# One subtraction and one clamp for eight heads in a Mamba-2 scan, and later stores of the second layer's weight pairs

## The chip, the cores and the metric

The kernel runs on one core of a Trainium2 chip. The metric is the device time of one execution in microseconds. Three runs of the kernel before took 3096.12, 3100.96 and 3102.59 us; the median is 3100.96.

## The reference

The model has two layers over 2048 tokens of width 1024. The first is a Mamba-2 mixer with 32 heads of width 64 in 4 groups and a state of 128; the second is multi-head latent attention with 16 heads, whose keys and values come from a latent of width 256. The part that the change touches in the first layer is the decay inside a chunk of the scan:

```python
cum = jnp.cumsum(dt_c * A_g, axis=1)
seg = cum[:, :, None] - cum[:, None, :]
L = jnp.exp(jnp.where(causal, seg, -jnp.inf))
CB = jnp.einsum('btgn,bsgn->btsg', C_c, B_c)
y_intra = jnp.einsum('btsg,btsgh,bsgh,bsghp->btghp', CB, L, dt_c, x_c)
```

The part that it touches of the second layer are that layer's weights: `w_dkv` (1024 x 288), `w_in` (1024 x 1408, the query latent and the gate), `w_ukv` (256 x 2048) and `w_uq` (384 x 1536). The reference multiplies with them in fp32.

## The kernel before

The kernel goes through the first layer in 16 items: four token blocks of 512 (b), and in each the four groups (g). An item has the projections (`xbc`, `zgate`), the scan (`ssd`) and the output projection (`outp`). The scan of one item is a generator that is advanced between the steps of the other parts, so that TensorE gets products of the projections between those of the scan. Then come the second layer's projections (`mla`), the attention (`attention`), whose TensorE order is written out by hand, and the last projection (`back`). Outside the attention a planner, which counts costs and priorities, sets the order of each engine's instructions when the kernel is built; on the chip each engine, SP's queue among them, keeps its order, and an instruction that waits holds up those behind it.

**The scan's differences (lines 829 to 845).** The scan of an item has four chunks of 128 tokens, 64 chunks in all. For each, SP fetches the rows of the cumulated decay of eight heads, spread over all partitions, into the tile E (tag `big`, two buffers, 128 x 8 x 128; line 831). VectorE subtracts from each head's 128 columns that head's column of `cum`, one value per partition, and clamps at zero from below (line 843, eight instructions). ScalarE takes the exponential (line 844), VectorE multiplies by CB (line 845), and TensorE takes E as weights of 16 products (line 870). Behind them lie y (lines 871 to 878), its square (880), a power of two from the square (883 to 885), the scaling of y (900) and its transpose (812).

**The second layer's weight pairs (lines 424 to 502).** Products with fp16 operands are made of pairs, a high and a low half, and the pairs of the second layer's weights are made in the background of the first layer's last two blocks, in 49 pieces of up to 512 columns. A piece is a raw load on SP (line 437, one piece ahead of its use), the high half on ScalarE and the low half on VectorE (`pair16`, lines 119 and 120), and a store of the pair to DRAM on SP (line 439). Raw weights and pairs share the five buffers of the tag `wraw`. `owed` holds pairs that are made and not yet stored. `make` runs most pieces; `value_weights` makes those of the value part of `kv_w_up`, which also yield a vector of powers of two, stored to `us_d` (line 493). Its pairs are stored at line 502, the first store of each of its two rounds at line 473, and the last store of all at line 461.

On the same SP queue stand the loads of the first layer's pairs (`wi_d`, line 230, and `wo_d`, line 694) and of the decay rows (line 831). ScalarE also empties the banks of `xbc` into `craw` (line 610), which frees the bank for the next products; line 781 is a small Exp for the chunks' end weights.

Of the kernel before, what the change touches and what calls it, by code (L numbers as in the profile page):

```python
# [10 lines left out]
F32 = mybir.dt.float32  # L11
# [5 lines left out]
ALU = mybir.AluOpType  # L17
# [4 lines left out]
P = 128  # L22
# [49 lines left out]
class Net:  # L72
# [352 lines left out]
    def second_weights(self):  # L425

        yield from self.second_powers()
        a = self.a
        owed = []

        def make(todo):
            raws = []
            for m, (src, gain, d) in enumerate(todo):
                while len(raws) < min(m + 2, len(todo)):
                    raws.append(self.t(self.wp, "wraw", [P, TB], bufs=WRAW))
                    ahead = todo[len(raws) - 1][0]
                    self.nc.sync.dma_start(raws[-1][:, :ahead.shape[1]], ahead)
                if owed:
                    self.nc.sync.dma_start(*owed.pop())
                n = src.shape[1]  # L440
                u = self.t(self.wp, "wraw", [P, 2, n], F16, bufs=WRAW)
                self.pair16(u[:, 0], u[:, 1], raws[m][:, :n], gain)
                owed.append((d, u))
                yield

        def rows(w, k, c0, n):
            return w[k * P:(k + 1) * P, c0:c0 + n]

        w_in = a["mla_w_in"]
        todo = [(rows(w_in, k, 384, TB), self.g1u[:, k:k + 1], self.wg_d[0][k]) for k in range(KD)]  # L450
        todo += [(rows(a["kv_w_down"], k, 0, 288), self.gku[:, k:k + 1], self.wd_d[k]) for k in range(KD)]
        todo += [(rows(w_in, k, 0, 384), self.g1u[:, k:k + 1], self.wq_d[k]) for k in range(KD)]
        todo += [(rows(a["kv_w_up"], k, n * TB, TB), self.gklu[:, k:k + 1], self.wu_d[n][k])
                 for n in range(2) for k in range(2)]
        yield from make(todo)
        yield from self.value_weights(owed)
        todo = [(rows(a["mla_w_uq"], k, n * TB, TB), self.gqu[:, k:k + 1], self.wu_d[4 + n][k])
                for n in (2, 0, 1) for k in range(3)]
        todo += [(rows(w_in, k, 384 + TB, TB), self.g1u[:, k:k + 1], self.wg_d[1][k]) for k in range(KD)]
        yield from make(todo)  # L460
        self.nc.sync.dma_start(*owed.pop())
        yield

    def value_weights(self, owed):

        nc, v = self.nc, self.nc.vector
        for n in range(2):
            cs = slice(1024 + n * 512, 1536 + n * 512)
            raw = [self.t(self.wp, "wraw", [P, TB], bufs=WRAW) for _ in range(2)]
            for k in range(2):  # L470
                nc.sync.dma_start(raw[k], self.a["kv_w_up"][k * P:(k + 1) * P, cs])
            if owed:
                nc.sync.dma_start(*owed.pop())
            yield
            u = [self.t(self.wp, "wraw", [P, TB], F32R, bufs=WRAW) for _ in range(2)]
            for k in range(2):
                nc.scalar.activation(u[k], raw[k], AF.Abs, scale=self.gkl[:, k:k + 1])
            yield
            ps = self.t(self.pp, "tr", [P, TB], bufs=4)
            for k in range(2):  # L480
                nc.tensor.matmul(ps, self.ones_r, u[k], start=k == 0, stop=k == 1)
            x = self.t(self.sp, "cacc", [P, TB], bufs=2)
            v.tensor_scalar(x, ps, TINY, None, ALU.max)

            e = self.t(self.sp, "craw", [P, TB], I32, bufs=3)
            v.tensor_scalar(e, x.bitcast(I32), 23, None, ALU.logical_shift_right)
            f = self.t(self.sp, "cacc", [P, TB], I32, bufs=2)
            v.tensor_scalar(f, e, -1, 264, ALU.mult, ALU.add)
            v.tensor_scalar(f, f, 23, None, ALU.logical_shift_left)
            v.tensor_scalar(e[0:1], e[0:1], -25, None, ALU.add)  # L490
            v.tensor_scalar(e[0:1], e[0:1], 23, None, ALU.logical_shift_left)
            v.tensor_scalar(e[0:1].bitcast(F32), e[0:1].bitcast(F32), self.gdown[0:1], None, ALU.mult)
            nc.sync.dma_start(self.us_d[n * 512:(n + 1) * 512], e[0:1, :].bitcast(F32))
            for k in range(2):
                nc.gpsimd.tensor_tensor(raw[k], raw[k], f.bitcast(F32), ALU.mult)
            yield
            for k in range(2):
                w = self.t(self.wp, "wraw", [P, 2, TB], F16, bufs=WRAW)
                self.pair16(w[:, 0], w[:, 1], raw[k], self.gklv[:, k:k + 1])
                owed.append((self.wu_d[2 + n][k], w))  # L500
                yield
                nc.sync.dma_start(*owed.pop())

    def second_powers(self):

# [283 lines left out]
    def ssd(self, b, g):  # L789

        nc, v, act = self.nc, self.nc.vector, self.nc.scalar.activation
        dt, cum, ecum, dec, wend, cumT = self.dtv[b]
# [27 lines left out]
        for c in range(4):  # L820
            s = slice(c * P, (c + 1) * P)
            h0 = c * H + g * 8
# [7 lines left out]
            E = self.t(self.sp, "big", [P, D], bufs=2).rearrange("p (h t) -> p h t", h=8)  # L830
# [8 lines left out]
                Ct = halves(pair("Ct", P, 2), CT[:, s])  # L839
            CB = self.t(self.sp, "CB", [P, P], bufs=2)  # L840
            v.tensor_tensor(CB, pb[:, P:2 * P], self.triu, ALU.mult)
            for h in range(8):
                v.tensor_scalar(E[:, h, :], E[:, h, :], cum[:, h0 + h:h0 + h + 1], 0.0, ALU.subtract, ALU.max)
            act(E, E, AF.Exp, scale=-1.0)
            v.tensor_tensor(E, E, CB.unsqueeze(1).to_broadcast([P, 8, P]), ALU.mult)
            yield
# [34 lines left out]
            if b:  # L881
                e = self.t(self.sm, "pwe", [P, 1], I32)
# [627 lines left out]
```

## Time and profile before

| | |
|---|---|
| median of three runs | 3100.96 us |
| profiled execution | 3099.32 us, its span 3097.2 us |
| mean granted TensorE clock | 0.995 |
| TensorE (matmul) busy | 2994.5 us, 97% |
| VectorE busy | 2330.1 us, 75% |
| ScalarE busy | 1936.4 us, 63% |
| GpSimd busy | 615.3 us, 20% |

Busy time is the union of the instructions' spans on an engine. A mean duration of one instruction also holds its passage through a pipeline, so that a row of instructions back to back takes less than their number times the mean. A wait is put down to the releaser that came last. Waits of SP are those of the queue that issues transfers.

### The profile page before, as it was taken

Reading aid. Unit: us, or ns where it says so; the run is one execution under the profiler, and the core shown is the slowest. Engines: PE = TensorE matmul, PEld = TensorE weight load, DVE = VectorE, ACT = ScalarE, POOL = GpSimd, SP = SyncE. Lnnn points to the kernel's source line nnn. Section 1 sums busy time; section 2 is a strip of 40 time slices with the busy share of each in tenths; the row PEclk is TensorE's granted clock in tenths of the full one; section 3 lists DMA queues with packets and bytes.
Section 4 is the critical chain, followed back from the end, with each engine's and each line's share of the span. In section 5 each row is a group of like instructions: output and inputs, shape, how many; then the busy total and the mean of one; then the engine's idle time right before and its main releaser. Section 6 shows DMA issues by size and latency. Waiting matters only on the chain.

```text
span 3097.2 us, 51355 instructions
## 1 busy us (share of the span) xinstructions
PE 2994.5 (97%) x17758; PEld 1759.2 (57%) x17758; DVE 2330.1 (75%) x5306; ACT 1936.4 (63%) x4920; POOL 615.3 (20%) x842
## 2 busy tenths in 40 slices
PE   7899999999999999999999999999999999999998
PEld 3466655555455554545555555456666666665777
DVE  7789887777777687797755453488888888888576
ACT  8777566665667656565534333388888888888422
POOL 0211122211222112222111212322122222222100
PEclk9999999999999999999999999999999999999999
DMA  8675436445454466364466555622223222232485
GB/s 298 221 235 181 151 106 220 129 158 163 153 191 162 131 207 222 121 199 145 145 214 197 194 173 170 197 49 60 55 56 67 54 58 57 54 88 75 130 261 158
DMA packets 205065, 457.11 MB, mean 148 GB/s; under 512 B 28114, under 2 KB 57554, under 8 KB 203364
## 3 DMA queue, kind: packets, MB, share of 16 engines
q1 hardware_dynamic: 176948, 375.94, 37.9%
q0 software_dynamic: 27856, 77.89, 9.8%
q8 instruction: 140, 2.29, 0.3%
q14 instruction: 121, 0.99, 0.1%
HBM read 340.99 MB, written 112.73 MB: 146 GB/s over the span
## 4 chain that ended last, share of the span: by engine, by line
PE 40%; DVE 5%; ACT 4%; issue 3%; DMA 2%; POOL 0%; SPq 0%; ACTq 0%; POOLq 0%; DVEq 0%
PE mm L88 7%; PE mm L90 6%; PE mm L89 6%; PE tr L1248 6%; PE tr L1259 3%; PE tr L1258 3%; PE tr L88 3%; PE tr L90 3%; PE tr L89 3%; ACT Pr L1233 2%; DVE PTs L120 1%; DMA os<-ri_d 1%; ACT PTs L119 1%; DVE mx L1221 1%; PE mm L1220 0%
## 5 line engine op out<-in xcount | busy, mean ns | idle before, releaser
L120 DVE SCALAR_TENSOR_TENSOR PTs<-tr,PTs 128x512 f16<-128x512 f32 (+3 forms) x640 | 374.2, 606 | 76.8 <-ACT PTs L119 69.7
L1233 ACT ACTIVATE Pr<-mm,nm 128x512 f32<-128x512 f32 (+2 forms) x631 | 394.2, 635 | 49.4 <-DVE nm L1225 44.9
L1221 DVE TENSOR_REDUCE mx<-mm 128x1 f32<-128x512 f32 (+2 forms) x631 | 373.1, 604 | 31.1 <-PE mm L90 28.3
L119 ACT ACTIVATE PTs<-tr 128x512 f16<-128x512 f32 (+3 forms) x640 | 329.4, 544 | 97.9 <-PE tr L1248 95.9
L1248 PE MATMUL tr<-pack,Pr 128*128 128x128 f32 x2176 | 317.5, 273 | 1.8 <-ACT Os L1265 1.4
L88 PE MATMUL mm<-xT,wsp 128*128 128x512 f16 x800 | 305.7, 382 | 7.9 <-ACT wsp L119 4.9
L89 PE MATMUL mm<-xT,wsp 128*128 128x512 f16 x800 | 304.6, 381 | 0.0
L90 PE MATMUL mm<-xT,wsp 128*128 128x512 f16 x800 | 303.6, 380 | 0.0
L1248 PEld LDWEIGHTS tr<-pack,Pr 128*128 128x128 f32 x2176 | 253.2, 141 | 68.9 <-ACT Os L1265 2.2
L88 PE MATMUL mm<-K,xT 96*128 96x512 f16 (+2 forms) x639 | 222.4, 348 | 27.5 <-ACT Pr L1233 24.0
L88 PE MATMUL mm<-wsp,xT 128*128 128x512 f16 (+1 forms) x640 | 232.0, 363 | 4.3 <-ACT craw L610 4.1
L89 PE MATMUL mm<-wsp,xT 128*128 128x512 f16 (+1 forms) x640 | 232.3, 363 | 3.0 <-DVE wsp L120 3.0
L89 PEld LDWEIGHTS <-xT 128*128 128x128 f16 (+1 forms) x1408 | 138.0, 98 | 168.1 <-issue 69.6
L616 DVE SCALAR_TENSOR_TENSOR cacc<-craw,pack,cacc 128x512 f32<-128x512 f32 x288 | 219.3, 790 | 18.0 <-ACT cacc L614 17.2
L90 PE MATMUL mm<-wsp,xT 128*128 128x512 f16 (+1 forms) x640 | 232.5, 364 | 0.0
L90 PE MATMUL mm<-K,xT 96*128 96x512 f16 (+2 forms) x639 | 221.8, 347 | 0.0
L89 PE MATMUL mm<-K,xT 96*128 96x512 f16 (+2 forms) x639 | 221.2, 346 | 0.0
L1258 PE MATMUL tr<-PTs,xT 128*128 128x512 f16 (+3 forms) x640 | 221.0, 347 | 0.1
L1259 PE MATMUL tr<-PTs,xT 128*128 128x512 f16 (+3 forms) x640 | 219.1, 347 | 0.0
L90 PEld LDWEIGHTS <-xT 128*128 128x128 f16 (+1 forms) x1408 | 136.9, 97 | 133.1 <-issue 5.7
L88 PEld LDWEIGHTS <-xT 128*128 128x128 f16 (+1 forms) x1408 | 137.7, 98 | 120.1 <-issue 8.5
L88 PE MATMUL mm<-wsp,yT 128*128 128x512 f16 (+1 forms) x512 | 197.4, 385 | 0.9 <-DVE sz L640 0.5
(456 smaller groups left out, 6795.8 us busy)
## 6 DMA issues: line engine op xcount, KB each, us to landing
wsp<-wi_d SPq DMA_DIRECT2D x96, 512.0 KB, 3.6
big<-cumT SPq DMA_DIRECT2D x64, 512.0 KB, 4.8
wraw<-in_ssm_w_out_dram SPq DMA_DIRECT2D x96, 256.0 KB, 3.6
wi_d<-wsp SPq DMA_DIRECT2D x32, 512.0 KB, 3.8
wsp<-wo_d SPq DMA_DIRECT2D x32, 512.0 KB, 3.5
wsp<-wu_d SPq DMA_DIRECT2D x28, 512.0 KB, 3.8
hx<-in_ssm_w_in_dram SPq DMA_DIRECT2D x48, 256.0 KB, 4.8
wraw<-in_ssm_w_in_dram SPq DMA_DIRECT2D x48, 256.0 KB, 4.4
```

The lines of the kernel that those rows point to most:

```text
L88: mm(out, l_hi, r_hi, start=start, stop=False)
L89: mm(out, l_hi, r_lo, start=False, stop=False)
L90: mm(out, l_lo, r_hi, start=False, stop=stop)
L119: self.nc.scalar.activation(hi, src, AF.Copy, scale=scale)
L120: self.nc.vector.scalar_tensor_tensor(lo, src, scale, hi, ALU.mult, ALU.subtract)
L616: nc.vector.scalar_tensor_tensor(acc, raw[:, k:k + TB], wk[k], acc, ALU.mult, ALU.add)
L1221: v.tensor_reduce(mx[:, n:n + 1], s[:, :w], AX.X, ALU.max)
L1233: nc.scalar.activation(x[:, :w], s[:, :w], AF.Exp, bias=nm, accum_out=sm[:, n:n + 1])
L1248: nc.tensor.transpose(pt[:, j * P:(j + 1) * P], st["P"][j][kb], self.ident)
L1258: nc.tensor.matmul(st["O"][:, c], vals[h][:, kb, :], u[:, 0], start=kb == 0, stop=False)
L1259: nc.tensor.matmul(st["O"][:, c], vals[h][:, kb, :], u[:, 1], start=False, stop=kb == nk - 1)
```

## The change

In the scan the eight instructions of line 843 become two for all eight heads: a subtraction of a tensor from a tensor, in which each head's column of `cum` is repeated over 128 elements, and a clamp at zero in place.

In `make`, a pair is stored only when more than one is owed, and then the oldest; before, the one owed was stored at the next piece. After the last piece all that are owed are stored. In `value_weights`, all owed pairs are stored once the raw loads of a round are issued; its own pairs are no longer stored right after they are made but with the next round or the next pieces; and the store of `us_d` is issued one step later.

```diff
-                if owed:
-                    self.nc.sync.dma_start(*owed.pop())
+                if len(owed) > 1:
+                    self.nc.sync.dma_start(*owed.pop(0))
...
         yield from make(todo)
-        self.nc.sync.dma_start(*owed.pop())
+        while owed:
+            self.nc.sync.dma_start(*owed.pop(0))
         yield
...
-            if owed:
-                nc.sync.dma_start(*owed.pop())
+            while owed:
+                nc.sync.dma_start(*owed.pop(0))
             yield
...
-            nc.sync.dma_start(self.us_d[n * 512:(n + 1) * 512], e[0:1, :].bitcast(F32))
             for k in range(2):
                 nc.gpsimd.tensor_tensor(raw[k], raw[k], f.bitcast(F32), ALU.mult)
             yield
+            nc.sync.dma_start(self.us_d[n * 512:(n + 1) * 512], e[0:1, :].bitcast(F32))
             for k in range(2):
                 w = self.t(self.wp, "wraw", [P, 2, TB], F16, bufs=WRAW)
                 self.pair16(w[:, 0], w[:, 1], raw[k], self.gklv[:, k:k + 1])
                 owed.append((self.wu_d[2 + n][k], w))
                 yield
-                nc.sync.dma_start(*owed.pop())
...
-            for h in range(8):
-                v.tensor_scalar(E[:, h, :], E[:, h, :], cum[:, h0 + h:h0 + h + 1], 0.0, ALU.subtract, ALU.max)
+            v.tensor_tensor(E, E, cum[:, h0:h0 + 8].unsqueeze(2).to_broadcast([P, 8, P]), ALU.subtract)
+            v.tensor_scalar(E, E, 0.0, None, ALU.max)
             act(E, E, AF.Exp, scale=-1.0)
```

## Rows read from the trace of the kernel before

**Rows 1.** Busy time by stretch: the scan layer, the pieces' part, the attention.
```profile
core 0: us, PE busy (x) PEld busy (x) DVE busy (x) ACT busy (x) POOL busy (x), PEclk, DMA share, GB/s
35.00:1560.00 1525.00, 1483.17 (x8902) 805.69 (x8901) 1208.33 (x2717) 972.08 (x2483) 312.05 (x381) 0.99 0.53 174
1090.00:1410.00 320.00, 306.57 (x1816) 157.32 (x1814) 265.17 (x608) 189.56 (x470) 70.67 (x79) 0.99 0.58 191
2010.00:3098.00 1088.00, 1046.07 (x6400) 707.56 (x6397) 879.00 (x2059) 774.65 (x2084) 199.29 (x289) 1.00 0.35 87
```

**Rows 2.** Waits of PE in 35 to 1560: total us, times, longest.
```profile
PE tr L812 <- ACT y L900: 9.1, 7, 2.7
PE mm L88 <- ACT craw L610: 5.8, 4, 3.1
```

**Rows 3.** Instruction groups by shape: busy us, mean ns, idle before.
```profile
L843 DVE TENSOR_SCALAR big<-big,d_cum 128x128 f32<-128x128 f32 x512 | 136.6, 314 | 38.5 <-DMA big<-cumT 38.3
...
L845 DVE TENSOR_TENSOR big<-big,CB 128x1024 f32<-128x1024 f32 x64 | 78.0, 1219 | 0.8
...
L578 DVE TENSOR_SCALAR hx<-hx,rsy 128x1024 f32<-128x1024 f32 x24 | 16.5, 749 | 0.2
...
L981 DVE TENSOR_SCALAR yt<-yt 128x512 f32<-128x512 f32 x4 | 1.7, 426 | 0.1
```

**Rows 4.** Timeline of DVE at 1349: start, us, instruction, idle before.
```profile
1349.22 1.66 DVE L843 TENSOR_SCALAR big<-big,d_cum 128x128 f32<-128x128 f32 x8 [1.83 <-DMA big<-cumT]
```

**Rows 5.** Timeline of DVE at 1190 to 1193.
```profile
1190.24 0.29 DVE L843 TENSOR_SCALAR big<-big,d_cum 128x128 f32<-128x128 f32 x1 [0.94 <-DMA big<-cumT]
...
1191.04 0.15 DVE L883 TENSOR_SCALAR pwe<-ms 128x1 int32<-128x1 int32 x1
...
1193.04 0.28 DVE L843 TENSOR_SCALAR big<-big,d_cum 128x128 f32<-128x128 f32 x1
```

**Rows 6.** Waits of SP's queue in 1048 to 1410.
```profile
SPq L439 <- DVE wraw L120: 37.3, 23, 5.2
SPq L502 <- DVE wraw L120: 7.5, 4, 4.0
SPq L493 <- DVE craw L492: 7.2, 1, 7.2
...
SPq L437 <- DMA wu_d<-wraw: 4.7, 5, 2.3
```

**Rows 7.** Timeline of SP's queue, 1324 to 1356.
```profile
1332.78 0.33 SPq L437 DMA_DIRECT2D wraw<-in_mla_w_uq_dram  x1
...
1342.98 0.45 SPq L831 DMA_DIRECT2D big<-cumT  x1
...
1354.86 0.38 SPq L437 DMA_DIRECT2D wraw<-in_mla_w_uq_dram  x1
```

**Rows 8.** Timeline of ACT, 1349 to 1352.
```profile
1349.95 0.72 ACT L119 ACTIVATE wraw<-wraw,gains 128x512 f16<-128x512 f32 x1 [2.21 <-DMA wraw<-in_mla_w_uq_dram]
1350.92 1.06 ACT L844 ACTIVATE big<-big 128x1024 f32<-128x1024 f32 x1 [0.25 <-DVE big L843]
1351.88 0.67 ACT L610 ACTIVATE craw<-mm,down 128x512 f32<-128x512 f32 x1
```

**Rows 9.** Timeline of PE, 1348 to 1356.
```profile
1352.60 0.38 PE L88 MATMUL mm<-wsp,xT 128*128 128x512 f16 x1 [3.15 <-ACT craw L610]
...
1354.49 0.38 PE L88 MATMUL mm<-wsp,xT 128*128 128x512 f16 x1 [0.44 <-ACT craw L610]
```

**Rows 10.** Timeline of ACT, 1117 to 1124.
```profile
1120.49 0.53 ACT L119 ACTIVATE wraw<-wraw,gains 128x288 f16<-128x288 f32 x1 [2.65 <-DMA wraw<-in_kv_w_down_dram]
```

**Rows 11.** Timeline of PE, 1120 to 1124.
```profile
1123.38 1.04 PE L870 MATMUL tr<-Xd,big 128*64 128x64 f32 x28 [2.44 <-issue]
```

**Rows 12.** The tile wraw in 1090 to 1410: who waited for it, landing times.
```profile
  ACT wraw L119: 33.8, 24
...
DMA to landing us min/median/max: 1.7/3.3/6.5
```

## The prediction

> **What bounds the kernel now.** I read the busy times by stretch first. In the scan layer, 35 to 1560 us, TensorE is busy 1483 of 1525 us at a granted clock of 0.99, VectorE 1208, ScalarE 972; in the attention stretch behind it, which the change doesn't touch, TensorE is busy 1046 of 1088 [rows 1]. So the scan layer is TensorE's: what the change can win in it is at most the 42 us in which TensorE stands idle there, and both edits lie on engines with room (VectorE idles 317 us of the stretch). The waits of TensorE come next: the largest two groups are a transpose that waits for ScalarE's last scaling of y (9.1 us in 7 waits) and a product that waits until ScalarE has emptied a bank into craw (5.8 us in 4) [rows 2]. Neither names the edited lines, so I looked for what stood in front of those ScalarE instructions in their queue. In the stretch in which the second layer's weights are made, 1090 to 1410, TensorE idles 13.4 us [rows 1], and its two longest waits there that lead to the edited work are followed below.
>
> **The scan's decay differences: operations.** The eight subtract-and-clamp instructions of a chunk have a mean duration of 314 ns [rows 3], but that is not what eight of them take: they are pipelined, and where nothing stands between them all eight end 1.66 us after the first has begun [rows 4]. They go, and one 128x1024 subtraction of two tensors comes, with a clamp of 128x1024 behind it that reads what the subtraction writes. The subtraction is in kind, width, type and in having one broadcast operand the multiplication of line 845, 1219 ns. The clamp has two near rows: 426 ns for 128x512 without a per-partition operand, 749 ns for 128x1024 with one [rows 3]. So a chunk costs between 1.22 + 0.43 = 1.65 us and 1.22 + 0.75 = 1.97 us in place of 1.66. I take the upper end, since that row has the width of the clamp: 0.31 us more for a chunk, 64 chunks, 20 us more of VectorE in a stretch where it idles 317.
>
> The Trainium skill ("VectorE: DVE Perf Modes", the section on the TRN2 errata) counts a VectorE instruction between SBUF operands as 58 cycles of 0.96 GHz plus its elements, divided by two where fp32 has one tensor operand. Worked out from that page as an estimate, eight small ones are 1.02 us and the new pair 1.72 us, so its rule speaks against the edit more strongly (0.70 us for a chunk, 45 us over 64), although the same section advises few large instructions over many small ones. The trace doesn't agree with it for the small ones, which take 1.66 us [rows 4]; by the page the scan half below would cost some 5 us in place of 2.
>
> **The scan half on the path.** The chain of a chunk is: cumT's rows land, differences, Exp, multiplication, TensorE's 16 products, y, the square, the power of two, the scaling, the transpose. TensorE waits for its end in 7 of 64 chunks [rows 2]; in the others it has other products, and VectorE's extra time is covered. If all 7 shift by 0.31 us the price is 2.2 us; I take 2. The bounds come from the other form in which the eight occur: the planner puts short instructions between them. From 1190.24 to 1193.32 the eight took 3.08 us, with the power-of-two chain of the chunk before (line 883) between [rows 5]. The new pair would give Exp its input 1.1 us sooner there, and 7 such chunks are worth -8 us. On the other side, line 883 stood behind one piece of 0.29 us; behind a subtraction of 1.22 us it would start 0.93 us later, and 7 times that is +6.5 us. The 38.3 us in which VectorE waits at the differences for cumT's rows [rows 3] stay whichever form waits.
>
> **The stores.** The same 49 stores of pairs and the same bytes are issued on SP; only their place changes. Before, the store of a piece stands right behind the next piece's load, and SP, which works in order, waits there for VectorE's low half: 37.3 us in 23 waits, 7.5 us in 4 at the value weights' own stores, and 7.2 us in one at the store of us_d [rows 6]. With one more piece between, the halves have long been made, so I put nearly all of the 37.3 and 7.5 at nothing, and the store of us_d behind one more piece. SP waits by themselves cost nothing; what stands behind them does: loads of raw weights, loads of cumT's rows and of the first layer's pairs.
>
> Where does that reach TensorE? First at 1352.60: it waited 3.15 us, then 0.44 us, for craw [rows 9]. ScalarE was free to empty the bank only at 1351.88, because it had stood 2.21 us at a raw weight that had not landed, and then did the Exp of a chunk [rows 8]. VectorE in turn had begun that chunk's differences at 1349.22 after 1.83 us of waiting for cumT's rows [rows 4], which SP had issued at 1342.98 [rows 7]. That is the train of loads that started only at 1332.78 [rows 7], when SP had come out of its 7.2 us at us_d [rows 6]. Starting it even 2 to 3 us sooner takes both waits away: -3.6 us. Second at 1123.38: TensorE stood 2.44 us [rows 11] because ScalarE had stood 2.65 us at a raw weight of the pieces, in front of a small Exp that the chunk needed [rows 10]. That load stood behind SP's store waits too: -2.4 us. Behind either the next late thing is the same ScalarE queue, which then has no gap; the other waits of the stretch (13.4 - 3.6 - 2.4 = 7.4 us) I leave. At the end, two stores in place of one are flushed; nothing stands behind them but first-layer loads, and I put that at nothing (0.4 us if SP were late then).
>
> What it costs is space. Five buffers hold raw weights and pairs alike. With one pair more held back, the next raw load finds free only the buffer of the piece just converted or that of a pair whose store was issued one piece before. Where that store hasn't landed, the wait comes back at the load (before, 4.7 us in 5 waits for one of the stored tensors [rows 6]). I take nothing for it in the forecast; its bound is the rival below.
>
> **Sum.** The profiled execution took 3099.3 us (span 3097.2). 3099.3 - 3.6 - 2.4 + 2 = 3095.3, so 3095, against the median of the three runs, 3101, a gain of 0.2%. Its own range, with half or none of the second term and the scan half between -2 and +4, is 3090 to 3101.
>
> **Rivals.**
> (a) *The ring of five becomes the bound: slower.* Place: the raw loads of the pieces. In the densest train nine loads went out between 1332.78 and 1354.86 [rows 7], one every 2.5 us, while a store's landing takes 3.3 us in the median [rows 12]. It decides where pieces follow each other closer than a store lands: then each load waits for the store before it, 0.8 us more, and 45 loads make 36 us. ScalarE stands at raw weights 33.8 us now [rows 12], and of that 5.6 us (3.15 + 2.44) came through to TensorE, one sixth; 36 us more would bring 6, neither gap would go, and with the scan's 2 the time is 3107 to 3108. For it: loads wait for stored tensors even now [rows 6]. Against it: the other free buffer, that of the piece just converted, may be taken, and over the whole stretch 49 pieces are made in 320 us, one in 6.5.
> (b) *The waits only change hands.* SP is free sooner, but the loads behind are held by TensorE's use of the buffers, or ScalarE meets its next late input: both gaps stay, the scan's 2 us are added: 3101. For it: both raw-weight waits shown end with a landing [rows 8, 10], and that the issue was late is my inference. Against it: SP's 7.2 us at us_d lead straight to the gap at 1352.60.
> (c) *The shorter path through the differences pays*: the -8 us above in place of +2: 3085. For it: interleaved runs of the eight as in [rows 5] exist. Against it: VectorE's work grows, and TensorE names none of these lines as its releaser.
>
> **How the numbers follow.** Forecast 0.48, (a) 0.24, (b) 0.16, (c) 0.12. A measurement of this kernel tells 0.2%, 6 us, from no change, so faster is below 3095 and slower above 3107. The forecast lies on that border: I give 0.27 of its 0.48 to faster and 0.21 to the same. With 0.11 of (c), faster is 0.38; with 0.19 of (a) and 0.03 of (b), slower is 0.22; the rest, 0.40, is the same. The range takes in (c) nearly and (a) with some room above: 3084 to 3112.
>
> **What would show it.** Right: the 1.83 us at the differences and the 2.21 us at the raw weight in that train gone, SP's waits at line 439 near nothing, the pair at 1.9 to 2.0 us per chunk, TensorE idle under 8 us between 1090 and 1410. Wrong: SP's waits at line 437 for stored tensors above 30 us and ScalarE's at raw weights above 50 (a); TensorE's idle time in 35 to 910 moved by more than 5 us, which only the scan half can do. If TensorE's idle time moves as much outside the named places as in them, the planner's new order and not these steps made the time, and the working above is wrong even where the time fits.

## The result and the profile after

The changed kernel took 3105.99 us in the median of 22 runs (3099.46 to 3111.57), the kernel before 3100.39 in as many beside it. The ratio is 1.0019, with a 95% interval of 1.0012 to 1.0025: 5.6 us slower, where 3095 and a gain had been forecast. The profiled execution took 3107.3 us (span 3105.5; before 3099.3 and 3097.2).

Busy time by stretch in the kernel after, for [rows 1]:

```profile
35.00:1560.00 1525.00, 1480.34 (x8868) 802.20 (x8867) 1219.18 (x2336) 971.86 (x2483) 323.81 (x381) 0.99 0.53 174
1090.00:1410.00 320.00, 304.84 (x1823) 157.23 (x1818) 264.88 (x518) 189.66 (x471) 71.23 (x80) 0.98 0.58 188
2010.00:3098.00 1088.00, 1054.42 (x6438) 711.95 (x6435) 878.72 (x2050) 775.96 (x2086) 202.22 (x293) 1.00 0.36 88
```

VectorE's busy time in the scan layer rose by 10.9 us (1208.3 to 1219.2), half of the 20 that I had counted. TensorE still idles 44.7 us there (1525 less 1480.3; before 41.8) and 15.2 in the pieces' part (before 13.4; forecast under 8). The third row holds 8 us more TensorE work than before because the layers ahead of it ended later. Idle time is not all of the loss: over the whole execution TensorE's 17758 products were busy 2999.2 us, before 2994.5, so that 4.7 of the 8.3 us by which the span grew are longer products. The mean granted clock of the profiled execution was 0.994, before 0.995.

TensorE's waits in 35 to 1560 after, for [rows 2]:

```profile
PE tr L812 <- ACT y L900: 12.9, 8, 4.5
PE mm L88 <- ACT craw L610: 6.2, 5, 2.9
```

The wait for y's last scaling grew from 9.1 to 12.9 us, and its longest from 2.7 to 4.5.

The differences by shape after, for [rows 3] (subtraction in line 842, clamp in 843):

```profile
L842 DVE TENSOR_TENSOR big<-big,d_cum 128x1024 f32<-128x1024 f32 x64 | 81.7, 1276 | 35.0 <-DMA big<-cumT 34.6
...
L843 DVE TENSOR_SCALAR big<-big 128x1024 f32<-128x1024 f32 x64 | 48.7, 761 | 0.2
```

Undisturbed, the two take 1.22 and 0.69 us (the medians are 1224 and 686 ns), so 1.91 for a chunk, as forecast.

SP's waits in 1048 to 1410 after, for [rows 6] (line 439 is the store of a pair, 437 the load of a raw weight, 497 the store of us_d, 472 the load of a raw value weight):

```profile
SPq L437 <- DVE wraw L120: 33.5, 12, 5.0
SPq L439 <- DVE wraw L120: 11.3, 9, 2.8
SPq L497 <- DVE craw L493: 7.5, 1, 7.5
...
SPq L472 <- DVE wraw L120: 4.9, 2, 3.7
SPq L437 <- DMA wd_d<-wraw: 4.7, 3, 1.7
```

The store's wait of 37.3 us shrank to 11.3, but the load that stands ahead of it took over 33.5 us of the same wait, for VectorE's low half (before, 3.5 us at the load). us_d still holds SP for 7.5 us. SP's waits at line 437 for stored tensors did not grow (15.1 us for all four tensors after, 15.5 before).

The tile wraw in 1090 to 1410 after, for [rows 12]:

```profile
  ACT wraw L119: 39.9, 31
...
DMA to landing us min/median/max: 1.9/3.5/6.5
```

ScalarE waited 39.9 us there, 33.8 before, and these waits are of several kinds. The largest of ScalarE's own list of waits in that stretch, for raw loads and for pairs on their way to DRAM:

```profile
ACT wraw L119 <- DMA wraw<-in_mla_w_in_dram: 10.6, 6, 3.5
ACT wraw L119 <- DMA wg_d<-wraw: 6.8, 5, 2.4
...
ACT wraw L478 <- DMA wu_d<-wraw: 4.0, 2, 2.0
ACT wraw L119 <- DMA wu_d<-wraw: 3.9, 3, 2.5
```

For raw loads line 119 waited 15.6 us, 17.1 before. For a buffer whose stored pair had not landed ScalarE waited 18.4 us (line 478, where the value weights are made, with it), 4.6 before. So raw weights come hardly earlier, and ScalarE has a new wait, for the stores.

The longest wait that TensorE has in the pieces' part after leads to the pair. Timelines of the kernel after at 1380 to 1385, VectorE first, then ScalarE, then TensorE:

```profile
1379.51 0.74 DVE L878 SCALAR_TENSOR_TENSOR y<-y,down,sz 128x512 f32<-128x512 f32 x1
...
1381.03 1.23 DVE L842 TENSOR_TENSOR big<-big,d_cum 128x1024 f32<-128x1024 f32 x1
1382.17 0.15 DVE L883 TENSOR_SCALAR pwe<-ms 128x1 int32<-128x1 int32 x1
...
1382.31 0.69 DVE L843 TENSOR_SCALAR big<-big 128x1024 f32<-128x1024 f32 x1
1382.91 0.15 DVE L884 TENSOR_SCALAR pwe<-pwe 128x1 int32<-128x1 int32 x1
...
1383.09 0.15 DVE L885 TENSOR_SCALAR pw<-pwe 128x1 int32<-128x1 int32 x1
```

```profile
1380.81 0.18 ACT L880 ACTIVATION_READ_ACCUMULATOR yt<-y 128x1 f32 x1
...
1382.99 1.04 ACT L258 ACTIVATE yt<-hx 128x1024 bf16<-128x1024 f32 x1
...
1384.03 0.70 ACT L900 ACTIVATE y<-y,pw 128x512 f32<-128x512 f32 x1
```

```profile
1384.78 1.11 PE L812 MATMUL tr<-pack,y 128*128 128x128 f32 x4 [4.50 <-ACT y L900]
```

Here is how these lines are read. The sum of squares is ready at 1380.99. Three VectorE instructions of 0.15 us each (883, 884, 885: the links, below) make the power of two from it, and ScalarE scales y by that. Of the next chunk's pair the subtraction stands ahead of the first link and the clamp between the first and the second, so the third link ends at 1383.24, 2.25 us after the sum. ScalarE begins the scaling only at 1384.03, when the instruction ahead of it in its queue (line 258) has ended. In the kernel before, a place of the same kind had single pieces between the links; the first link is the 1191.04 of [rows 5], and this is the timeline of VectorE behind it:

```profile
1191.17 0.28 DVE L843 TENSOR_SCALAR big<-big,d_cum 128x128 f32<-128x128 f32 x1
1191.37 0.15 DVE L884 TENSOR_SCALAR pwe<-pwe 128x1 int32<-128x1 int32 x1
...
1191.69 0.15 DVE L885 TENSOR_SCALAR pw<-pwe 128x1 int32<-128x1 int32 x1
```

There the three links take 0.80 us from the first start to the last end, against 1.07 in the kernel after. Counted from the sum's end at 1189.53, this place of the kernel before is no shorter (2.31 us), because its first link stood behind a piece that waited for cumT's rows [rows 5] and an addition of 0.68 us (line 896). Elsewhere in the kernel before nothing stands between the links, and they follow each other closer still:

```profile
1346.02 0.15 DVE L883 TENSOR_SCALAR pwe<-ms 128x1 int32<-128x1 int32 x1 [0.19 <-ACT yt L880]
1346.21 0.15 DVE L884 TENSOR_SCALAR pwe<-pwe 128x1 int32<-128x1 int32 x1
1346.40 0.15 DVE L885 TENSOR_SCALAR pw<-pwe 128x1 int32<-128x1 int32 x1
```

So a place by itself decides little, and the sum over all of them is what counts. I summed, over the 48 chunks that have links (those of the second to the fourth block of tokens), the time from the sum's end to the third link's end: 64.0 us before, 101.4 after. The median from one link's start to the next one's is 0.26 us before and 0.66 after.

The wait of 4.50 us cost more than itself. The granted clock in 1384 to 1390 (columns as in [rows 1]), and two products of 512 columns, one in that stretch and one behind it:

```profile
1384.00:1390.00 6.00, 5.22 (x15) 2.36 (x16) 4.48 (x17) 5.01 (x10) 0.00 (x0) 0.50 0.27 90
```

```profile
1386.12 0.63 PE L89 MATMUL mm<-wsp,xT 128*128 128x512 f16 x1
...
1390.60 0.38 PE L88 MATMUL mm<-wsp,yT 128*128 128x512 f16 x1
```

TensorE had stood idle, and then the clock was at the lower of its two levels, 1.2 GHz in place of 2.4. The products behind the wait took 0.63 us each and started 0.43 us apart, later 0.38 and 0.22.

### The profile page after: what moved, and what is told of

Read it like the earlier page. It is cut to its first block, busy times and chain, and to the rows that moved or that the text cites. A ratio compares the mean times of both kernels' runs of the same rounds, so it can differ in the third digit from the quotient of the medians.

```text
span 3105.5 us, 50950 instructions
## 1 busy us (share of the span) xinstructions
PE 2999.2 (97%) x17758; PEld 1759.9 (57%) x17758; DVE 2339.7 (75%) x4922; ACT 1936.1 (62%) x4920; POOL 627.0 (20%) x842
## 4 chain that ended last, share of the span: by engine, by line
PE 58%; DVE 15%; ACT 7%; DMA 6%; issue 4%; SPq 1%; POOL 1%; ACTq 0%; DVEq 0%; POOLq 0%
PE mm L88 12%; PE mm L90 11%; PE mm L89 11%; PE tr L1248 6%; DVE cacc L616 3%; PE tr L1259 3%; PE tr L1258 3%; PE tr L88 3%; PE tr L89 3%; PE tr L90 3%; ACT Pr L1233 2%; DMA big<-cumT 2%; DVE PTs L120 1%; PE tr L870 1%; DMA os<-ri_d 1%
```

## The experiments

All times are medians beside runs of the kernel before on the same chip; brackets are 95% intervals of the ratio to it. The kernel before took 3098.37 us beside e1, e2, s1 and s2, 3099.17 beside e3, n2, n4 and v2, 3100.82 beside the c kernels, 3101.00 beside the g kernels and h1, and 3099.53 beside b1 and b2. The ratio is not the quotient of the two medians; for most kernels the two agree within an us, for h1 they are 2.8 us apart. A loss in us goes by the ratio, unless two kernels are set against each other by their medians.

**The two halves by themselves.** `e1_scan` is the kernel before with the scan half alone, `e2_stores` with the store half alone:

```
e1: -  for h in range(8): v.tensor_scalar(E[:, h, :], ..., ALU.subtract, ALU.max)
    +  v.tensor_tensor(E, E, cum[...].to_broadcast([P, 8, P]), ALU.subtract)
    +  v.tensor_scalar(E, E, 0.0, None, ALU.max)
e2: -  if owed: dma_start(*owed.pop())
    +  if len(owed) > 1: dma_start(*owed.pop(0))     (and the rest of the store edit)
```

> Only the scan edit: one subtraction and one clamp for eight heads; the stores as in the kernel before. Theory A (the pair costs VectorE 1.91 us for a chunk where eight in a row took 1.66, and comes in larger pieces, and TensorE pays for it): slower than before by 4 to 7 us, ratio 1.0013 to 1.0023, with the gaps of TensorE before 1090 us, where no weight pieces are made, grown by 3 us or more. Theory B (the stores did it, by the waits that went from the store to the next load): within 2 us of before.

> Only the store edit; the eight instructions for eight heads stay. Theory B (the stores did it): slower by 4 to 7 us, TensorE's idle time between 1090 and 1410 us grown by 3 us or more. Theory A (the scan did it): within 2 us of before, SP's waits at the stores (37 us) found again at the loads, TensorE's idle time there 11 to 15 us as before.

e1: 3105.12 us, 1.0020 [1.0010, 1.0029]. e2: 3097.02, 0.9993 [0.9984, 1.0002]. The whole loss is the scan half's, 6.2 us; the store half is not told from no change. In its profile TensorE idles 10.1 us in 1090 to 1410, 13.4 before [rows 1]:

```profile
1090.00:1410.00 320.00, 309.87 (x1859) 159.45 (x1856) 266.36 (x609) 191.23 (x480) 71.63 (x79) 0.99 0.59 192
```

**Length of the differences.** `s1_noclamp` leaves the clamp out, with another scale in the Exp; `s2_twoclamps` makes it twice:

```
s1: -  v.tensor_scalar(E, E, 0.0, None, ALU.max)
    -  act(E, E, AF.Exp, scale=-1.0)
    +  act(E, E, AF.Exp, scale=-0.001)
s2: +  v.tensor_scalar(E, E, 0.0, None, ALU.max)     (a second time)
```

> The scan edit without its clamp, and with the exponent scaled by 1/1000 so that it stays finite (the decay is not computed rightly). VectorE has 1.22 us for a chunk in place of 1.91 (before: 1.66). Theory A (VectorE's time for the differences): faster than the scan edit alone by 6 us or more and faster than before by 2 us or more. Rival (the planner's new order, whatever the pair costs): no such step, the time lies anywhere within 6 us of the scan edit alone.

> The scan edit with the clamp done twice: VectorE has 2.6 us for a chunk. Theory A: slower than the scan edit alone by 5 us or more, about the step from no clamp to one. Rival (the planner's order): not in line, within 3 us of the scan edit alone or faster than it.

s1: 3102.75, 1.0016 [1.0007, 1.0024]; s2: 3112.83, 1.0048 [1.0036, 1.0061]. One subtraction of 1.22 us is shorter than the eight pieces' 1.66 and still slower, so length alone does not explain the loss, and theory A, which had this kernel faster than before, fails here. The second clamp, 0.7 us more per chunk, costs another 8.7 us (some 3 of them go with a lower clock, see below), so length counts too.

**Smaller pieces, and controls.** `e3_halves` makes subtraction and clamp for four heads at a time; `n2_cb_later` moves one instruction of the kernel before (CB's product) behind the eight, and `n4_ahead12` draws the weight loads 12 places ahead in place of 10, to see what another order alone does:

```
e3: +  for h in (0, 4):
    +      v.tensor_tensor(E[:, h:h + 4, :], ..., ALU.subtract)
    +      v.tensor_scalar(E[:, h:h + 4, :], E[:, h:h + 4, :], 0.0, None, ALU.max)
n4: -  AHEAD = 10
    +  AHEAD = 12
```

> The scan edit in two halves: subtraction and clamp for four heads, then for the other four; the stores as before. VectorE has some 2.2 us for a chunk (four instructions of 0.7 and 0.4 us) against 1.9 of the pair and 1.7 of the eight, but no piece is longer than those that it has anyway. Theory T1 (the size of a piece in VectorE's order hurts: short instructions that TensorE's next work hangs on stand behind 1.2 us): at least half of the loss comes back, 2 us or less above before. Theory A (VectorE's time for a chunk): slower than the pair, 9 us or more above before. Rival (the planner's new order, whatever the pieces): anywhere within 6 us of the pair.

> A control: the kernel before with the small multiplication that makes CB written after the eight instructions in place of before them. The work and its pieces are the same; only the planner's order changes here and there. Theory T1 and A: within 2 us of before. Rival (an order by chance is worth some us): 3 us or more off on either side.

> A second control: the kernel before with the weight loads drawn 12 places ahead in place of 10. The work and its pieces are the same; only the planner's order changes. Theory T1 and A: within 2 us of before. Rival (an order by chance is worth some us): 3 us or more off on either side.

e3: 3114.33, 1.0047 [1.0033, 1.0060]; n2: 3100.88, 1.0001 [0.9993, 1.0010]; n4: 3098.63, 0.9999 [0.9991, 1.0007]. Both controls stay where they were: two orders that differ a little cost nothing, which does not rule out a larger change of order. That halves are worse than wholes is against the simple rule that a smaller piece blocks less (theory T1), although the links' sum is 79.5 us, less than the 100.1 of the pair in e1. Theory A had named 9 us or more; a part of the 15 us goes with the clock (below).

**Half the heads on ScalarE.** `v2_split` gives every second head's subtract-and-clamp to ScalarE (with cum negated where it is made):

```
+  if h % 2: act(E[:, h, :], E[:, h, :], AF.Relu, bias=cum[:, h0 + h:h0 + h + 1])
+  else: v.tensor_scalar(E[:, h, :], ..., ALU.add, ALU.max)
```

> The kernel before with the eight differences shared between two engines: four heads on VectorE as before, four on ScalarE as a rectified sum with the negated cumulated decay as its bias. VectorE has 0.85 us for a chunk in place of 1.66, in small pieces, ScalarE 1.05 us more. Theory A (VectorE's time near a chunk's end is what TensorE's waits for y hang on): 2 to 6 us faster than before. Rival (ScalarE, which empties the banks, becomes the late one): 2 us or more slower.

v2: 3110.54, 1.0033 [1.0020, 1.0046]. This is the rival's side. ScalarE, which has the other half of the work now, also makes the y that TensorE waits for: that wait is 14.1 us (9.1 before), though the links' sum is 59.8.

**An edge in the planner's order.** The differences of a chunk are queued only behind the three links of the chunk before, as pair (`c1_edge_pair`), as eight (`c3_edge_eight`), as eight with the store half (`c4_edge_stores`) and as pair with two clamps (`c5_edge_twoclamps`):

```
+  with self.tc.issue_after(self.link.ins) if self.link else ExitStack():
       ... the differences ...
-  v.tensor_scalar(pw[:, c:c + 1].bitcast(I32), e, 23, None, ALU.logical_shift_left)
+  self.link = v.tensor_scalar(pw[:, c:c + 1].bitcast(I32), e, 23, None, ALU.logical_shift_left)
```

> The scan edit (stores as before) with one edge for the planner: the pair of a chunk is issued on VectorE only behind the three short instructions (power of two) of the chunk before, so that no piece of the pair stands between these. VectorE does the same work. Theory C (the loss is the three links' wait behind the pair, which the planner puts between them): links' time from the square's end to the power of two down from 100 us to 65 or less, TensorE's wait for the scaled y down from 15 to 10 us or less, and the time within 2 us of the kernel before. Theory A (VectorE's time for the pair itself): stays 5 to 8 us above before.

> The kernel before, with the eight instructions for eight heads, and the same edge: the eight of a chunk only behind the three links of the chunk before. Theory C: links' time below its 64 us, and the time at before or up to 4 us faster. Rival (the eight fill the pauses between the links at no cost, and an edge only delays them): at before or up to 4 us slower.

> The eight with the edge and the store edit. Theory C, and the stores alone at about 2 us faster: the sum of both, 0 to 6 us faster than before. If the time is above before, the edge costs what the links save.

> The pair with a second clamp and the edge: VectorE has 2.6 us for a chunk, none of it between the links. Theory C (links): most of the 14.5 us of the same kernel without the edge gone, 6 us or less above before. Theory A (VectorE's time): 10 us or more above before, by the 0.7 us of each chunk.

c1: 3102.37, 1.0008 [0.9999, 1.0017]; c3: 3098.49, 0.9993 [0.9985, 1.0002]; c4: 3097.40, 0.9989 [0.9979, 0.9998]; c5: 3105.41, 1.0018 [1.0009, 1.0027]. The links' sum falls to between 39 and 41 us in all four. The edge helps the eight as well, though, so the pair still lies 3.9 us over the eight (medians of c1 and c3), and two clamps 6.9: the links' place is not all. c4 is the one version whose interval lies below the kernel before, by 0.11%, and its clock was higher by about as much (below).

**The links off the path.** In `g1_free_eight`, `g2_free_pair` and `g3_free_twoclamps` y is scaled by a constant, so that no part of the chunk waits for the links; `h1_two_links_pair` makes the power of two in two links:

```
g:  -  act(y, y, AF.Copy, scale=pw[:, c:c + 1])
    +  act(y, y, AF.Copy, scale=2.0 ** -20)
h1: +  v.tensor_scalar(e, ms[:, c:c + 1].bitcast(I32), 24, 23, ALU.logical_shift_right, ALU.logical_shift_left)
    +  v.tensor_scalar(pw[:, c:c + 1].bitcast(I32), e, -1, (127 + 63 + 8) << 23, ALU.mult, ALU.add)
```

> The kernel before, with one thing left out: ScalarE scales y by a constant in place of the chunk's power of two, so the three short VectorE links are still made, but nothing of the chunk's chain waits for them (y's size is then another one; no instruction is added or taken away). It is the base for the two kernels beside it. Both theories: 0 to 5 us under the kernel before (ratio 0.9985 to 1.000), since TensorE's 9.1 us of waiting for that scaling can shrink.

> The scan edit alone, with the same thing left out as in g1_free_eight. Theory C (the pair costs because it comes between the links, and y's scaling waits for them): with nothing waiting for the links the pair costs next to nothing, 0 to 2 us over g1_free_eight (ratios 0.0006 apart at most). Rival L (the pair costs because the differences themselves end 0.25 us later in each chunk, or because VectorE is busier): 4 to 7 us over g1_free_eight (0.0013 to 0.0023), as much as the scan edit cost in the whole kernel (6.2).

> As g2_free_pair with a second clamp (2.6 us of VectorE per chunk in place of 1.91). Theory C: 1 to 5 us over g1_free_eight, well under the 14.5 us that the second clamp version cost with the links on the path. Rival L: 9 to 15 us over g1_free_eight.

> The scan edit alone, with two links in place of three: the first shifts right by 24 and left by 23, the second multiplies by -1 and adds the shifted constant, with the same result to the bit. Theory C: there is one boundary less at which a piece of the pair can come between, so a third to a half of the 6.2 us goes: 3101 to 3103.5, ratio 1.0006 to 1.0014 (and up to 0.2 us x 7 less from the shorter chain itself). Rival L: as the scan edit alone, ratio 1.0016 to 1.0022.

g1: 3101.14, 1.0000 [0.9991, 1.0009]; g2: 3103.03, 1.0005 [0.9996, 1.0014]; g3: 3112.94, 1.0043 [1.0030, 1.0055]; h1: 3102.81, 1.0015 [1.0005, 1.0025]. With nothing waiting for the links the pair costs 1.9 us (medians of g2 and g1) in place of 6.2, as theory C said, but the intervals of the two overlap; two clamps cost 11.8 more than the eight, which only rival L said. h1's time lies between the two theories. Its links' sum is 60.3 us and TensorE's wait for the scaling 8.4, both below the kernel before's, and its ratio still shows a loss: the links' time is not all.

**Where it arises.** The profiles have a landmark, the last evacuation of the z gate of each item. From that of the first item to that of the fourth, all in the first block of tokens, which has no links, the seven profiles with eight differences took 262.3 to 265.5 us and the five with the pair 265.7 to 268.1. So the last two kernels have the pair in the first block's 16 chunks only (`b1_pair_first`) and in the other 48 only (`b2_pair_rest`):

```
b1: +  if b == 0: the pair, else: the eight
b2: +  if b: the pair, else: the eight
```

> The pair in the first 16 chunks only (the first block of tokens, up to 351 us), the eight in the other 48. The first block has no power-of-two links, and VectorE is busy 242 of the 276 us from 84 to 360 in the kernel before. From the z gates of the first item to those of the fourth, the seven profiles with eight differences took 262.3 to 265.5 us, the five with the pair 265.7 to 268.1. Theory C alone (only the links' place costs): no change, ratio 0.9995 to 1.0005, and that stretch at 263 to 265. Theory Q (in any stretch in which VectorE's queue is full, what stands behind the pair in it comes later, links or not): 3 to 4 us slower, ratio 1.0010 to 1.0013, and that stretch at 266 to 268.

> The other way round: the eight in the first 16 chunks, the pair in the 48 that have links. Theory C alone: all of the scan edit's 6 us, ratio 1.0017 to 1.0023. Theory Q: 2 to 3 us, ratio 1.0006 to 1.0010, with the first stretch at 263 to 265, and TensorE's wait for y's last scaling at 13 to 15 us as in the scan edit alone (9.1 before).

b1: 3103.39, 1.0011 [1.0002, 1.0019], and that stretch took 266.8 us. b2: 3106.40, 1.0023 [1.0014, 1.0031], and the stretch took 263.4. Either part is slower by itself. Together they would make 1.0034, e1 has 1.0020; with intervals of about 0.0009 each that is at the edge of the error. Theory C alone had no change for b1, and theory Q 2 to 3 us for b2, so neither fits both kernels by its time.

TensorE's waits in 84 to 1560 in b2_pair_rest (its line 904 is the scaling of y):

```profile
PE tr L812 <- ACT y L904: 15.0, 7, 4.1
...
PE mm L89 <- DVE wsp L120: 3.0, 1, 3.0
```

The same in b1_pair_first:

```profile
PE tr L812 <- ACT y L904: 8.8, 7, 2.4
```

The wait for the scaling grew in b2, and in b1 it is as before (9.1). In b2's profile it made no more idle time, though: other waits shrank (that for craw from 5.8 to 2.6), and TensorE is busy in the scan layer for the 1483.17 us of the kernel before [rows 1]:

```profile
35.00:1560.00 1525.00, 1483.17 (x8861) 804.65 (x8860) 1218.02 (x2431) 973.37 (x2481) 324.18 (x381) 0.99 0.53 174
```

What grew is the time of the products. Busy times of the whole execution, first the kernel before, then b2:

```profile
PE 2994.5 (97%) x17758; PEld 1759.2 (57%) x17758; DVE 2330.1 (75%) x5306; ACT 1936.4 (63%) x4920; POOL 615.3 (20%) x842
```

```profile
PE 3003.4 (97%) x17758; PEld 1762.9 (57%) x17758; DVE 2338.9 (75%) x5018; ACT 1938.2 (62%) x4920; POOL 626.7 (20%) x842
```

That is 8.9 of the 9.0 us by which this profile's span is longer, at a granted clock of 0.991 against 0.995.

The second row of b2's waits, a wait for the low half of a weight pair that VectorE makes in the first block, has the 3.0 us of the kernel before; b1 has 4.1 there (below). The links' sums agree: 103.7 us in b2, 62.8 in b1.

What fills VectorE in the first block is seen in the busy times of 84 to 360 us (columns as in [rows 1]), first the kernel before, then b1:

```profile
84.00:360.00 276.00, 262.07 (x1566) 152.99 (x1565) 242.27 (x502) 205.46 (x495) 57.43 (x66) 0.98 0.60 198
```

```profile
84.00:360.00 276.00, 260.12 (x1553) 150.16 (x1552) 245.10 (x437) 204.71 (x493) 61.24 (x66) 0.98 0.59 196
```

VectorE is busy 242 of the 276 us, 88%, against 79% in the whole layer [rows 1]. The four largest rows of TensorE's waits for VectorE there in b1:

```profile
PE mm L89 <- DVE wsp L120: 4.1, 1, 4.1
PE tr L146 <- DVE ss L192: 2.4, 2, 2.1
PE mm L90 <- DVE wsp L120: 1.9, 2, 1.0
PE tr L812 <- DVE xT L120: 1.2, 1, 1.2
```

They are 9.8 us together with a fifth of 0.2; the kernel before has 6.0 (3.0 + 1.7 + 1.0 + 0.3) in four rows of that kind. Waits for ScalarE went the other way there, 7.8 to 5.9, so the waits show 1.9 of b1's 3 to 4 us; the rest was not traced to a row.

**The clock in these runs.** Each run has its mean granted TensorE clock on record, and the kernels differ in it. Among runs of one and the same kernel, a clock lower by 0.001 goes with 2.3 us more (a straight line through the 339 runs whose clock is on record, each taken against the mean of its kernel). The last column takes that off; it is an estimate, good to about 1.5 us (2 for e3 and s2).

| kernel | mean clock | kernel before beside it | mean time over before, us | the same at a like clock, us |
|---|---|---|---|---|
| e1, pair | 0.9943 | 0.9942 | 6.5 | 6.7 |
| b1, pair in the first 16 chunks | 0.9946 | 0.9946 | 3.4 | 3.5 |
| b2, pair in the other 48 | 0.9929 | 0.9946 | 7.1 | 3.4 |
| e3, halves | 0.9918 | 0.9945 | 14.6 | 8.5 |
| s2, two clamps | 0.9928 | 0.9942 | 15.3 | 12.1 |
| c1, pair with the edge | 0.9947 | 0.9941 | 2.2 | 3.4 |
| c3, eight with the edge | 0.9947 | 0.9941 | -1.9 | -0.5 |
| c4, eight with the edge, later stores | 0.9953 | 0.9941 | -3.6 | -0.8 |
| g2, pair, links off the path | 0.9951 | 0.9938 | 1.3 | 4.2 |
| g1, eight, links off the path | 0.9946 | 0.9938 | -0.2 | 1.7 |

So e1's loss does not go with the clock, and b1 and b2 make it up in two shares that are not told apart. Some 6 of e3's 15 us go with the clock, and what is left is not told from the pair's loss. c4's gain is not shown to be more than its clock. Whether longer waits bring the lower clock about, as the timeline around 1384 suggests, was not tested.

## Why the prediction was wrong

The forecast was 3095.3, the changed kernel took 3106.0. Of these 10.7 us the scan half has 4.2 (+2 forecast, +6.2 measured in e1) and the store half 3.8 (-6.0 forecast, -2.2 by e2's ratio). The rest is that the profiled execution, from which the sum started, was 1.1 us under the median, and the error of the two halves.

**The scan half: the step that failed.** The operation was sized rightly, 1.91 us per chunk against a forecast of 1.9 to 2.0. What failed is "I take 2": seven chunks shifted by 0.31 us each, the rest covered. I read from [rows 5] that pieces and links are interleaved, but priced the pair as a longer version of the block in [rows 4], and treated the interleaved form as an edge. The runs show two costs in the place of that term. In the 48 chunks that have links the pair holds these up: their sum went from 64.0 to 101.4 us, and TensorE's wait for the scaling from 9.1 to 15.0 in the kernel that has the pair in these chunks only. With the links kept together, or with nothing waiting for them, the pair costs 3.9 and 1.9 us. In the first block, which has no links, it costs 0.11%. At a like clock either part, the 48 chunks and the first 16, is some 3.5 us by the estimate above. The same edit with a shorter pair (s1) still loses, which the price by length cannot give.

A bound of the prediction comes near the measured +6.2: line 883 behind a subtraction of 1.22 us, 0.93 us later, times 7, +6.5 us. That is luck. It prices the links alone, and about half of the loss has no link in it; and in [rows 5] an addition of 0.68 us (line 896) stood between the piece and line 883, which I had passed over.

**The cover was an average.** "In the others it has other products, and VectorE's extra time is covered" rested on 317 idle us of VectorE in 1525. In the first block VectorE idles only 34 of 276 us, and b1 lost 0.11% there, without a link. The Trainium skill ("VectorE: DVE Perf Modes", the section on the TRN2 errata) advises few large instructions over many small ones; no run here shows a gain from it, and e1's eight-into-two lost 0.20%. VectorE's busy time rose by 10.9 us, not by my 20. Nor was it the 45 that I had worked out from the Trainium skill's row of 58 cycles, of which the same section says that it comes out too low for a single instruction.

**The store half: -3.6 and -2.4 forecast, about -2 measured.** The step "I put nearly all of the 37.3 and 7.5 at nothing" failed at the load: a load whose buffer is still being read for the low half waits just as the store did, 33.5 us. e2's ratio stands for -2.2 us, with an interval from -5.0 to +0.6, so it is not told from nothing and the forecast -6.0 lies outside. In e2's profile the second named wait, 1123.38 [rows 11], is down to 0.28 us, and the first gave way to another:

```profile
1121.86 1.15 PE L870 MATMUL tr<-Xd,big 128*64 128x64 f32 x32 [0.28 <-issue]
```

```profile
1348.71 0.38 PE L88 MATMUL mm<-wsp,xT 128*128 128x512 f16 x1 [2.09 <-DMA wraw<-in_mla_w_uq_dram]
```

ScalarE had stood 2.06 us at a late raw weight there, which is how rival (b) had it. In the changed kernel the second wait is gone from the list, and the first is found again, with ScalarE held just before (its row first):

```profile
1356.69 0.72 ACT L119 ACTIVATE wraw<-wraw,gains 128x512 f16<-128x512 f32 x1 [2.49 <-DMA wu_d<-wraw]
```

```profile
1358.74 0.38 PE L88 MATMUL mm<-wsp,xT 128*128 128x512 f16 x1 [2.86 <-ACT craw L610]
```

It was 3.15 us and is 2.86, and ScalarE stood 2.49 us not at a raw weight but at a buffer whose stored pair had not landed. That is rival (a), the ring of five, at this place: ScalarE's waits for stored pairs rose from 4.6 to 18.4 us. The signs that were named for (a) did not come (SP's waits at line 437 for stored tensors 15.1 us, under the 30), and e2 shows no loss by it. The 33.8 us of [rows 12], which I had read as raw weights, hold 17.1 us of raw loads; and its 3.3 us of landing are of loads and stores together. A sixth buffer was not tried. Rival (c), a shorter path through the differences, did not show: ScalarE waited 36.1 us for them after and 32.4 before.

**Signs named ahead.** Right by the list: the pair's duration. Wrong by the list: TensorE's idle time in 1090 to 1410 (15.2 us, under 8 forecast), SP's waits at line 439 (11.3, near nothing forecast), and the waits in that train (1.95 us at the raw weight, 2.21 before; 3.19 at the differences, 1.83 before). TensorE's idle time in 35 to 910 moved by 2.5 us (busy 849.3 to 846.8), under the bound of 5 that was to condemn the scan half: the bound was too wide, and it looked at idle time alone, where over half of the longer span was in longer products. The last sign came as well: in the named places TensorE's idle time fell by 3.2 us, and in the rest of the layer it rose by 6.0.

**What stays open.** The split of the 6 us between links and first block is known only to within the intervals (b1 3.4 us by the ratio 1.0011, b2 7.1, of which the lower clock has some 4). Why the clock was lower in b2 and e3, what the pair costs beside the links in the later blocks, and which row carries the rest of b1's loss, were not settled. A larger change of the planner's order as a cause is not excluded. The links on GpSimd were not tried.

## What to carry to other kernels

Many small instructions on an in-order engine are also places at which short dependent work can come in between; before fusing them, look in the timeline for what stands between them now, and price the fused form by how long that work is held up, not by its own length alone. Take an engine's cover from the stretch in which the edit runs, not from the layer's mean. Where kernels differ by 0.1 or 0.2%, compare the granted clock of all their runs, and TensorE's busy time beside its idle time, before a wait in one profile is called the cause. Where a store is issued later so that it needn't wait, look at what the next load's buffer is still used for: the wait goes to whichever instruction reaches it first.

## What was not expected of the hardware

Eight VectorE instructions of 128x128 take 0.28 to 0.29 us each by their records, but where they stand in a row all eight end in 1.66 us [rows 4], and dependent links of 0.15 us start 0.33 us apart with a piece and one other short instruction in each gap (1191.04, 1191.37, 1191.69), and 0.19 apart with nothing between them (1346.02, 1346.21, 1346.40): the two together hold a link up by 0.14 us, half of the piece's recorded length. GpSimd's copy of the state (line 806) has a median of 1278 ns before and 1275 after, but its longest grew from 1963 to 3016 ns, and VectorE's wait for it from 22.2 to 34.9 us. The time does not follow it: g2 has 33.2 us of it and e3, the slowest kernel, 17.3.
